# Fill products, tile forms, transfer order and norm-product places at the start and the block boundaries of a two-layer hybrid network

## The chip, the cores and the metric

The kernel runs on one core of one Trainium2 chip. The core has five engines that this text names by the profile's short names: PE (TensorE, matrix products), DVE (VectorE), ACT (ScalarE), POOL (GpSimd, idle here) and SP (SyncE, which issues every transfer here). Each works through its own queue in order, and they wait for each other by semaphores. The metric is device time in microseconds (us), the median of the timed runs; lower is better.

## The reference, cut to what matters

Two layers of a network with a latent sequence `x` and a context sequence `ctx`, 256 tokens of 1024 channels each. Each layer runs a feed-forward block, a mixer (a gated linear recurrence in layer 0, retention in layer 1) and a second feed-forward block. Ahead of each of them a norm is taken, scaled and shifted by vectors that come from a small product with the condition `c`:

```python
def modulate(h, shift, scale):
    return h * (1 + scale) + shift

def ada_mod(cond, w, b):
    m = jax.nn.silu(cond) @ w + b
    return jnp.split(m[..., None, :], N_MOD, axis=-1)
...
    for i in range(DEPTH):
        mx = ada_mod(c, mod_w[i], mod_b[i])
        mc = ada_mod(c_ctx, mod_w[i], mod_b[i])
        x = x + MACARON_W * mx[2] * swiglu(modulate(rms_norm(x, norm_g[i, 0]), mx[0], mx[1]),
                                           ffn_w_in[i, 0], ffn_w_out[i, 0])
        ...
        hx = modulate(rms_norm(x, norm_g[i, 1]), mx[3], mx[4])
        ...
        x = x + mx[5] * yx
        x = x + MACARON_W * mx[8] * swiglu(modulate(rms_norm(x, norm_g[i, 2]), mx[6], mx[7]),
                                           ffn_w_in[i, 1], ffn_w_out[i, 1])
    return rms_norm(x, final_g)
```

In the last layer only `x` is carried on after the mixer.

## The kernel before, in words

**Layout.** Channels lie on the 128 partitions, so `x` is 8 tiles (chunks) of 128x512: 256 context columns and 256 latent columns. All 371 weight tiles of 128x1024 (eight 128x128 blocks each) come in through SP in the order of use. A weight tile is split into a high part `whi` (ACT, L112) and a low part `wlo` (DVE, L138; some tiles are named `hhi`, `hlo`, since they are kept longer), and so is the input (`h`: ACT L348 writes the high half, DVE L354 the low half). A block of the product is three PE products: high by high (L142), high by low input (L143), low by high (L144).

**Modulation vectors.** `mod_order` lists 144 tiles of 128x1024, each worth 128 entries of one of nine vectors of a layer. A tile in form "V" is taken by DVE: two multiply-and-sum passes over 1024 columns (L242), one for each condition, and a small finishing operation (L265). A tile in form "P" is taken by PE: eight products of two columns each (L237, 16 entries in the trace), finished by two small operations on DVE (L262, L263). Vector 0 is the shift and vector 1 the scale of the first norm.

**The start** (`run`). SP issues the condition, the identity, `x` (8 transfers), then modulation and weight tiles. PE spreads the condition (L195), DVE sums the squares of `x` (`sq_acc`), PE sums them over the partitions (L296, in `stat`), DVE makes the inverse root in ten small operations (ends at L316), PE spreads it over the partitions (L329, `bcast`; "the broadcast" below). Then each chunk k of the normed input `h` is made by `h_chunk`: DVE (L346, scale), ACT (L348, shift and high half), DVE (L354, low half). A chunk needs its tile of vector 0 and of vector 1.

**The first product group** (`ffn` through `first_group`). Six accumulators stay open while PE goes through the eight chunks: 6 blocks of 3 products of 512 columns for a chunk, 18 in all (a "chunk's block" below). After chunk k's block a hook takes the two modulation tiles of chunk k+2 and makes `h` of chunk k+2.

**The block boundaries** (`boundary`, `out_proj`). After a block's output product the next norm is made while PE goes on. The context half's norm is made beside the latent half's output product; the latent half's `stat` and `bcast` lie in hooks of the next block's first group, which goes through the chunks twice with four accumulators: first the context columns (range 0), then the latent columns (range 1), 12 products of 256 columns for a chunk and range. A hook (r, k) runs after chunk k of range r. Four boundaries in the program have this form. Two, in the last layer after the mixer and at the program's end, carry only the latent half ("latent boundaries" below): there PE has nothing else to do, and `warm` fills it with products of a zero tile (L323), ten ahead of the broadcast, and six behind it at the first of the two.

**Order of the queues.** The order on each engine is that of the code. `w(key)` splits new weight tiles: the high part is issued at a tile's first block, the low part (`w_low`) when the blocks of the tile's second half begin. A small operation that is "pending" (`flush`) is issued by the next `h_chunk`.

Of the kernel before, what the change touches and what calls it, by code (L numbers as in the profile page):

```python
# [9 lines left out]
F32 = mybir.dt.float32  # L10
# [6 lines left out]
P = 128  # L17
# [26 lines left out]
def mod_order():  # L44

    out = []
    for k in range(KD):
        out.append((0, 0, k, "V", True))
        out.append((0, 1, k, "P", True))
# [25 lines left out]
class Kernel:  # L75
# [41 lines left out]
    def w(self, key, n=1):  # L117
# [9 lines left out]
        if o >= 4 or t == 0:  # L127
            self.w_low()
# [98 lines left out]
    def _tick(self):  # L227
# [6 lines left out]
        if form == "P":  # L234
# [4 lines left out]
            self.mod_finish(layer, idx, k, k + 1, 0, ps[:, 0:2])  # L239
        else:  # L240
# [5 lines left out]
            if (layer, idx) == (0, 0):  # L246
# [5 lines left out]
    def mod_finish(self, layer, idx, k0, k1, c0, src=None):  # L252
# [3 lines left out]
        ng = self.vec("ng").rearrange("p (l i k c) -> p l i k c", l=2, i=3, k=KD)  # L256
        if src is None:
            src = m
        else:
            src = src.rearrange("p (k c) -> p k c", k=k1 - k0)[:, :, c0:2]  # L260
# [15 lines left out]
    def sq_acc(self, st, d, c0, c1):  # L276

        nc = self.nc
# [4 lines left out]
        else:  # L283
            s = self.tmp("sq")
            nc.scalar.activation(s[:, :w], self.x[d][:, c0:c1], AF.Square)
            self.pend.append(lambda: nc.vector.tensor_tensor(st["acc"][:, :w], st["acc"][:, :w], s[:, :w],  # L286
                                                             ALU.add))

    def stat(self, s, ng, scale, between=None):
# [4 lines left out]
        ps = self.psum()  # L294
        for j in range(ng):
            nc.tensor.matmul(ps[:, j:j + 1], s[:, j * P:(j + 1) * P], self.ones, start=True, stop=True,  # L296
                             skip_group_check=True)
        if between:
            between()
# [59 lines left out]
    def out_proj(self, acts, key, layer, gidx, halves, st=None, hooks=None, tick=0, hold=False):  # L359
# [6 lines left out]
        for hi_, (c0, c1) in enumerate(halves):  # L366
# [14 lines left out]
            for d in range(KD):  # L381
# [6 lines left out]
                if st is not None and d:  # L388
                    self.sq_acc(st[hi_], d - 1, c0, c1)
                for c in range(2):  # L390
# [13 lines left out]
    def boundary(self, acts, key, layer, gidx, nl, nn, x_only=False, hold=False):  # L404
# [3 lines left out]
        if x_only:  # L408
            st = [{}]
            self.out_proj(acts, key, layer, gidx, [(T, 2 * T)], st=st)  # L410
            y = self.stat(st[0]["acc"], 2, 1.0 / D)
            self.warm(10)
# [19 lines left out]
        def hc(c, *ks):  # L432
            for k in ks:
# [4 lines left out]
        return {(0, 0): lambda: hc(0, 5, 6), (0, 1): lambda: (hc(0, 7), stat(1)), (0, 5): lambda: (bc(1), hc(1, 0)),  # L438
                (0, 6): lambda: hc(1, 1, 2), (0, 7): lambda: hc(1, 3, 4), (1, 0): lambda: hc(1, 5),
                (1, 1): lambda: hc(1, 6), (1, 2): lambda: hc(1, 7)}  # L440
# [528 lines left out]
    def run(self):  # L969
        nc, tc = self.nc, self.tc  # L970
        with ExitStack() as ctx:
# [27 lines left out]
            for k in range(1, 4):  # L999
                self.mod_prefetch(2 * k + 2, True)  # L1000
                self.w_fetch(k + 1)
# [5 lines left out]
            todo = self.spread_c()  # L1007
            st = {}
            for k in range(KD):
                self.sq_acc(st, k, 0, 2 * T)  # L1010
            self.flush()
            for o, ps in todo:
                nc.scalar.activation(o, ps, AF.Copy)
            y = self.stat(st["acc"], 4, 1.0 / D, self._tick)
            self._tick()
# [161 lines left out]
```

## Time and profile before

| what | before |
|---|---|
| median of 3 runs | 1885.56 us (1885.52 to 1885.7) |
| profiled execution, its own time | 1887.7 us |
| its span | 1885.9 us |
| mean granted PE clock | 0.991 |
| PE busy | 1857.2 us (98%), 10278 products |
| DVE busy | 1283.8 us (68%) |
| ACT busy | 718.2 us (38%) |
| HBM read | 274.80 MB, 146 GB/s over the span |

The profiled execution is 2.1 us longer than the median of the runs, and 1.8 us of its time lie outside its span. PE counts as busy while it works on anything, the fill included. The granted clock is 1 at 2.4 GHz and 0.5 at 1.2 GHz.

### The profile page before, as it was taken

How to read it: one execution, taken by the hardware profiler on the slowest of the kernel's cores; microseconds unless marked ns; L12 is line 12 of the kernel's file. 1: busy time of each engine (PE TensorE's matmuls, PEld its weight loads, DVE VectorE, ACT ScalarE, POOL GpSimd, SP SyncE). 2: the span in 40 equal slices, each digit the busy share in tenths (PEclk: the TensorE clock that was granted, in tenths of full speed). 3: DMA queues.
4: the chain of work that ended last, by engine and by line, in shares of the span. 5: the costliest groups of instructions: out<-in, count | busy, mean ns of one | idle time of the engine just before them, and what ended most of it. 6: DMA issues, size and time to landing. Idle time of an engine off the chain costs nothing.

```text
span 1885.9 us, 25731 instructions
## 1 busy us (share of the span) xinstructions
PE 1857.2 (98%) x10278; PEld 1621.5 (86%) x10278; DVE 1283.8 (68%) x2110; ACT 718.2 (38%) x984; POOL 0.2 (0%) x4
## 2 busy tenths in 40 slices
PE   8999999999999899999999999999999999999998
PEld 7888888897888888888889888888898899989997
DVE  7877697676899975767577655455576465675555
ACT  3322222248989342222224322222244243344442
POOL 0000000000000000000000000000000000000000
PEclk8999999999999999999999999999999999999999
DMA  8355454422322244454452445444324333355552
GB/s 319 127 211 187 167 189 181 145 90 79 100 90 90 79 157 168 158 185 172 143 172 94 154 150 187 145 171 178 102 80 150 124 123 118 97 160 182 176 186 101
DMA packets 77736, 277.52 MB, mean 147 GB/s; under 512 B 8752, under 2 KB 10032, under 8 KB 77616
## 3 DMA queue, kind: packets, MB, share of 16 engines
q1 hardware_dynamic: 77616, 275.88, 42.5%
q8 instruction: 80, 1.31, 0.3%
q14 instruction: 40, 0.33, 0.1%
HBM read 274.80 MB, written 1.05 MB: 146 GB/s over the span
## 4 chain that ended last, share of the span: by engine, by line
PE 92%; DVE 5%; ACT 1%; issue 1%; DMA 0%; SPq 0%; ACTq 0%; DVEq 0%
PE ps L142 30%; PE ps L144 30%; PE ps L143 30%; PE ps L237 1%; DVE x L393 1%; DVE wlo L138 1%; DVE hlo L138 1%; DVE h L354 0%; ACT h L348 0%; DVE acc L286 0%; PE ps L323 0%; PE ps L329 0%; PE ps L296 0%; DVE ht L346 0%; DMA x<-xt 0%
## 5 line engine op out<-in xcount | busy, mean ns | idle before, releaser
L142 PE MATMUL ps<-h,whi 128*128 128x512 f32 (+1 forms) x1824 | 641.1, 352 | 0.0
L144 PE MATMUL ps<-h,wlo 128*128 128x512 f32 (+1 forms) x1824 | 639.7, 351 | 1.2 <-DVE wlo L138 1.2
L143 PE MATMUL ps<-h,whi 128*128 128x512 f32 (+1 forms) x1824 | 640.3, 351 | 0.5 <-DVE h L354 0.5
L138 DVE TENSOR_TENSOR wlo<-wraw,whi 128x1024 fp32r<-128x1024 f32 x349 | 417.7, 1220 | 78.3 <-ACT whi L112 78.2
L112 ACT ACTIVATE whi<-wraw 128x1024 fp32r<-128x1024 f32 x349 | 357.3, 1050 | 275.8 <-PE ps L143 225.6
L144 PEld LDWEIGHTS ps<-h,wlo 128*128 128x128 f32 x1824 | 345.8, 190 | 47.7 <-DVE wlo L138 1.9
L143 PEld LDWEIGHTS ps<-h,whi 128*128 128x128 f32 x1824 | 345.9, 190 | 46.5 <-DVE h L354 1.6
L142 PEld LDWEIGHTS ps<-h,whi 128*128 128x128 f32 x1824 | 345.9, 190 | 44.9 <-ACT whi L112 0.3
L242 DVE SCALAR_TENSOR_TENSOR junk<-modraw,cB 128x1024 bf16<-128x1024 f32 x240 | 293.1, 1221 | 4.6
L393 DVE SCALAR_TENSOR_TENSOR x<-ps,M,x 128x256 f32<-128x256 f32 x296 | 132.5, 479 | 160.7 <-PE ps L144 160.3
L157 ACT ACTIVATE A<-sil 128x512 fp32r<-128x512 f32 (+1 forms) x88 | 50.9, 579 | 474.0 <-DVE sil L486 474.0
L142 PE MATMUL ps<-A,whi 128*128 128x512 f32 (+1 forms) x608 | 217.9, 358 | 0.0
L143 PE MATMUL ps<-A,whi 128*128 128x512 f32 (+1 forms) x608 | 217.9, 358 | 0.0
L144 PE MATMUL ps<-A,wlo 128*128 128x512 f32 (+1 forms) x608 | 217.9, 358 | 0.0
L486 DVE TENSOR_TENSOR sil<-ps,sil 128x512 f32<-128x512 f32 (+1 forms) x88 | 54.8, 623 | 159.8 <-PE ps L144 151.9
L144 PEld LDWEIGHTS ps<-A,wlo 128*128 128x128 f32 x608 | 114.9, 189 | 16.9
L143 PEld LDWEIGHTS ps<-A,whi 128*128 128x128 f32 x608 | 114.9, 189 | 16.9
L142 PEld LDWEIGHTS ps<-A,whi 128*128 128x128 f32 x608 | 114.9, 189 | 16.7
L158 DVE TENSOR_TENSOR A<-sil,A 128x512 fp32r<-128x512 f32 (+1 forms) x88 | 55.1, 626 | 56.7 <-ACT A L157 56.7
L485 ACT ACTIVATE sil<-ps 128x512 f32<-128x512 f32 (+1 forms) x88 | 47.3, 538 | 80.4 <-PE ps L144 79.9
L348 ACT ACTIVATE h<-ht,M 128x256 fp32r<-128x256 f32 x88 | 42.4, 504 | 91.5 <-DVE ht L346 91.5
L142 PE MATMUL ps<-A,hhi 128*128 128x256 f32 x192 | 54.8, 285 | 0.0
(171 smaller groups left out, 2065.3 us busy)
## 6 DMA issues: line engine op xcount, KB each, us to landing
wraw<-w SPq DMA_DIRECT2D x371, 512.0 KB, 4.3
modraw<-modw SPq DMA_DIRECT2D x144, 512.0 KB, 4.3
x<-xt SPq DMA_DIRECT2D x8, 256.0 KB, 4.9
mask<-mask SPq DMA_DIRECT2D x4, 512.0 KB, 6.0
out<-fin SPq DMA_DIRECT2D x8, 128.0 KB, 1.8
cs<-rope SPq DMA_DIRECT2D x1, 256.0 KB, 2.6
vecs<-vecs SPq DMA_DIRECT2D x1, 251.0 KB, 7.4
ident<-ident SPq DMA_DIRECT2D x1, 64.0 KB, 2.0
```

The source lines that it names most:

```text
L112: nc.scalar.activation(hi, raw, AF.Copy)
L138: self.nc.vector.tensor_tensor(lo, raw, hi.bitcast(F32), ALU.subtract)
L142: mm(ps, whi, xhi, start=first, stop=False, skip_group_check=True)
L143: mm(ps, whi, xlo, start=False, stop=False, skip_group_check=True)
L144: mm(ps, wlo, xhi, start=False, stop=last, skip_group_check=True)
L157: self.nc.scalar.activation(hi, src, AF.Copy)
L158: self.nc.vector.tensor_tensor(lo, src, hi.bitcast(F32), ALU.subtract)
L242: nc.vector.scalar_tensor_tensor(self.junk, raw, 1.0, self.cB[:, c, :], op0=ALU.mult, op1=ALU.mult, accum_out=M[:, idx, k, c:c + 1])
L348: nc.scalar.activation(h[:, 0, a:b], tt, AF.Identity, bias=M[:, 3 * n, k, c:c + 1])
L393: nc.vector.scalar_tensor_tensor(self.x[d][:, a0:a1], ps[:, a0 - c0:a1 - c0], M[:, gidx, d, c:c + 1], self.x[d][:, a0:a1], op0=ALU.mult, o ...
L485: nc.scalar.activation(s[:, :w], pa[:, c0:c1], AF.Silu)
L486: nc.vector.tensor_tensor(s[:, :w], pg[:, c0:c1], s[:, :w], ALU.mult)
```

## The change

**Forms.** Of the first 16 modulation tiles, vectors 0 and 1 of chunks 0 to 7 in turn, vector 0 was all "V" and vector 1 all "P". Now both tiles of chunks 0 and 1 are "P", chunks 2 to 5 are as before, and both tiles of chunks 6 and 7 are "V": eight of each form, as before. Finishing a tile of vector 1 takes one DVE operation (L260) in place of two, with `mb1` made ahead.

**The start.** On PE, 10, 3, 1 and 4 fill products stand between the spreading, the tile products, the norm products and the broadcast; the four tile products of chunks 0 and 1 all stand ahead of the first weight product, and the first of them ahead of the norm products. Of the transfers, modulation tiles 0 to 4 come ahead of weight tile 1 and 5 to 7 ahead of tile 2; in the hooks, tiles are fetched further ahead.

**The boundaries.** At the four two-half boundaries the latent `stat` moves from hook (0, 1) to (0, 2), the broadcast and the first chunk from (0, 5) to (0, 6), and the later chunks each by one hook. At the last chunk of an output product the pending sum of squares is issued ahead of the update of `x`. At the two latent boundaries the last chunk's squares are no longer added by DVE but summed by PE beside the others (two products accumulate), and the fill ahead of the broadcast is six instead of ten.

```diff
 def mod_order():
-        out.append((0, 0, k, "V", True))
-        out.append((0, 1, k, "P", True))
+        out.append((0, 0, k, "V" if k > 1 else "P", True))
+        out.append((0, 1, k, "P" if k < 6 else "V", True))
...
 def w(self, key, n=1):
-        if o >= 4 or t == 0:
+        if o >= 4:
             self.w_low()
...
 def _tick(self, late=None):
-            self.mod_finish(layer, idx, k, k + 1, 0, ps[:, 0:2])
+            f = lambda: self.mod_finish(layer, idx, k, k + 1, 0, ps[:, 0:2])
+            f() if late is None else late.append(f)
...
-            if (layer, idx) == (0, 0):
+            if layer == 0 and idx < 2:
                 self.mod_finish(layer, idx, k, k + 1, 0)
...
 def mod_finish(self, layer, idx, k0, k1, c0, src=None):
+        if layer == 0 and idx == 1:
+            nc.vector.tensor_scalar(m[:, 0], m[:, 0] if src is None else src, self.mb1[:, k0:k0 + 1],
+                                    ng[:, layer, 0, k0, 0:1], op0=ALU.add, op1=ALU.mult)
+            return
...
 def sq_acc(self, st, d, c0, c1):
+            if d == KD - 1 and st.get("two"):
+                st["last"] = s
+                return
...
 def stat(self, s, ng, scale):
+        parts = s if isinstance(s, list) else [s]
         for j in range(ng):
-            nc.tensor.matmul(ps[:, j:j + 1], s[:, j * P:(j + 1) * P], self.ones, start=True, stop=True,
-                             skip_group_check=True)
+            for i, s in enumerate(parts):
+                nc.tensor.matmul(ps[:, j:j + 1], s[:, j * P:(j + 1) * P], self.ones, start=i == 0,
+                                 stop=i == len(parts) - 1, skip_group_check=True)
...
 def out_proj(...):
                     self.sq_acc(st[hi_], d - 1, c0, c1)
+                    if d == KD - 1:
+                        self.flush()
...
 def boundary(...):
-            st = [{}]
+            st = [{"two": True}]
...
-            y = self.stat(st[0]["acc"], 2, 1.0 / D)
-            self.warm(10)
+            y = self.stat([st[0]["acc"], st[0]["last"]], 2, 1.0 / D)
+            self.warm(6)
...
-        return {(0, 0): lambda: hc(0, 5, 6), (0, 1): lambda: (hc(0, 7), stat(1)), (0, 5): lambda: (bc(1), hc(1, 0)),
-                (0, 6): lambda: hc(1, 1, 2), (0, 7): lambda: hc(1, 3, 4), (1, 0): lambda: hc(1, 5),
-                (1, 1): lambda: hc(1, 6), (1, 2): lambda: hc(1, 7)}
+        return {(0, 0): lambda: hc(0, 5, 6), (0, 1): lambda: hc(0, 7), (0, 2): lambda: stat(1), (0, 6): lambda: (bc(1), hc(1, 0)),
+                (0, 7): lambda: hc(1, 1, 2), (1, 0): lambda: hc(1, 3, 4), (1, 1): lambda: hc(1, 5),
+                (1, 2): lambda: hc(1, 6), (1, 3): lambda: hc(1, 7)}
...
 def run(self):
-            for k in range(1, 4):
-                self.mod_prefetch(2 * k + 2, True)
-                self.w_fetch(k + 1)
+            self.mod_prefetch(5, True)
+            self.w_fetch(2)
+            self.mod_prefetch(8, True)
...
             todo = self.spread_c()
+            self.warm(10)
...
-            y = self.stat(st["acc"], 4, 1.0 / D, self._tick)
-            self._tick()
+            late = []
+            self._tick(late)
+            y = self.stat(st["acc"], 4, 1.0 / D)
+            self.warm(3)
+            self._tick(late)
+            self.warm(1)
             rb = self.bcast(y, 4)
+            self.warm(4)
+            self.mb1 = self.const.tile([P, KD], F32, name="mb1")
...
+            for f in late:
+                f()
...
             h0(0)
             self.w_low()
+            self._tick()
+            self._tick()
+            h0(1)
...
                     if k + 2 < KD:
+                        self.mod_prefetch(min(2 * k + 10, 2 * KD), True)
                         self._tick()
                         self._tick()
                         h0(k + 2)
```

Three places show what moves. The lines of the changed kernel are 1 to 24 higher than those of before.

PE at the start, before, from the spreading (L195) to the first weight products (L142 to L144); L237 is the product of a modulation tile:

```order
L195 MATMUL ps<-ident,cT 128x128 x16
L296 MATMUL ps<-ones,acc 128x1 x4
L237 MATMUL ps<-cT,modraw 128x2 x8
L329 MATMUL ps<-ident,rs_y 128x128 x4
L237 MATMUL ps<-cT,modraw 128x2 x8
L142 MATMUL ps<-h_241,whi 128x512
```

The same with the change, from behind the ten fill products (L333; each is a pair of rows, and of three, one and four pairs one stands here); L238 is the tile product, L308 the norm product, L339 the broadcast:

```order
L238 MATMUL ps<-cT,modraw 128x2 x8
L308 MATMUL ps<-ones,acc 128x1 x4
...
L333 MATMUL ps<-warm_sb 128x512
L238 MATMUL ps<-cT,modraw 128x2 x8
L333 LDWEIGHTS warm_sb
L333 MATMUL ps<-warm_sb 128x512
L339 MATMUL ps<-ident,rs_y 128x128 x4
...
L238 MATMUL ps<-cT,modraw 128x2 x16
L142 MATMUL ps<-h_269,whi 128x512
```

Four tile products stand ahead of the first weight product where two stood, and the norm products stand behind the first of them.

DVE in the first group, before, for the two last chunks (`x_93`, `x_94`); L242 is one pass over a tile in form V:

```order
L242 SCALAR_TENSOR_TENSOR junk,M_85<-modraw,cB 128x1024 x2
L265 TENSOR_TENSOR M_85<-M_85,vecs 128x2
L262 SCALAR_TENSOR_TENSOR M_85<-ps,vecs 128x2
L263 TENSOR_TENSOR M_85<-M_85,vecs 128x2
L346 SCALAR_TENSOR_TENSOR ht<-x_93,M_85,ps 128x256 x2
L354 SCALAR_TENSOR_TENSOR h_514<-ht,M_85,h_514 128x256 x2
L242 SCALAR_TENSOR_TENSOR junk,M_85<-modraw,cB 128x1024 x2
L265 TENSOR_TENSOR M_85<-M_85,vecs 128x2
L262 SCALAR_TENSOR_TENSOR M_85<-ps,vecs 128x2
L263 TENSOR_TENSOR M_85<-M_85,vecs 128x2
L346 SCALAR_TENSOR_TENSOR ht<-x_94,M_85,ps 128x256 x2
L354 SCALAR_TENSOR_TENSOR h_563<-ht,M_85,h_563 128x256 x2
```

And with the change (L244 is the pass, L356 and L364 make `h`):

```order
L244 SCALAR_TENSOR_TENSOR junk,M_85<-modraw,cB 128x1024 x2
L271 TENSOR_TENSOR M_85<-M_85,vecs 128x2
L244 SCALAR_TENSOR_TENSOR junk,M_85<-modraw,cB 128x1024 x2
L260 TENSOR_SCALAR M_85<-M_85,mb_260,vecs 128x2
L356 SCALAR_TENSOR_TENSOR ht<-x_93,M_85,ps 128x256 x2
L364 SCALAR_TENSOR_TENSOR h_538<-ht,M_85,h_538 128x256 x2
L244 SCALAR_TENSOR_TENSOR junk,M_85<-modraw,cB 128x1024 x2
L271 TENSOR_TENSOR M_85<-M_85,vecs 128x2
L244 SCALAR_TENSOR_TENSOR junk,M_85<-modraw,cB 128x1024 x2
L260 TENSOR_SCALAR M_85<-M_85,mb_260,vecs 128x2
L356 SCALAR_TENSOR_TENSOR ht<-x_94,M_85,ps 128x256 x2
L364 SCALAR_TENSOR_TENSOR h_579<-ht,M_85,h_579 128x256 x2
```

Each of these two chunks has two tiles on DVE ahead of it where it had one.

DVE at a two-half boundary, before, from the end of the latent inverse root to the first latent chunks (`x0_87`, `x1_88`; the number behind a name is the buffer's):

```order
L316 SCALAR_TENSOR_TENSOR rs_y_3162<-rs_t_3161,rs_y_3162 128x2
L138 TENSOR_TENSOR hlo_3177<-wraw_2886,hhi_3176 128x1024
L138 TENSOR_TENSOR wlo_3207<-wraw_3111,whi_3206 128x1024
L346 SCALAR_TENSOR_TENSOR ht_3237<-x0_87,M0_85,ps_3234 128x256
L346 SCALAR_TENSOR_TENSOR ht_3257<-x1_88,M0_85,ps_3234 128x256
L354 SCALAR_TENSOR_TENSOR h0_3046<-ht_3237,M0_85,h0_3046 128x256
```

With the change:

```order
L326 SCALAR_TENSOR_TENSOR rs_y_3195<-rs_t_3194,rs_y_3195 128x2
L138 TENSOR_TENSOR hlo_3175<-wraw_2902,hhi_3174 128x1024
L138 TENSOR_TENSOR wlo_3223<-wraw_3127,whi_3222 128x1024
L356 SCALAR_TENSOR_TENSOR ht_3270<-x0_87,M0_85,ps_3267 128x256
L138 TENSOR_TENSOR wlo_3253<-wraw_3172,whi_3252 128x1024
L356 SCALAR_TENSOR_TENSOR ht_3286<-x1_88,M0_85,ps_3267 128x256
L364 SCALAR_TENSOR_TENSOR h0_3062<-ht_3270,M0_85,h0_3062 128x256
```

A weight tile's low part, which stood behind the second chunk, now stands between the first chunk's scaling and its low half (`h0`). On PE the broadcast stands one chunk later, with one chunk of range 0 (12 products) instead of two between it and the first product of range 1.

## Rows read from the trace of the kernel before

**Rows 1.** Stretches of the start: length, busy and count per engine, PEclk, DMA.

```profile
7.80:11.40 3.60, 0.00 (x1) 0.00 (x0) 2.55 (x4) 3.32 (x6) 0.00 (x0) 1.00 1.02 381
14.20:17.50 3.30, 3.30 (x17) 3.30 (x17) 2.40 (x13) 1.06 (x1) 0.00 (x0) 0.50 1.04 416
22.80:28.50 5.70, 5.70 (x15) 4.44 (x15) 4.92 (x12) 2.30 (x4) 0.00 (x0) 0.50 0.66 261
28.60:29.60 1.00, 1.00 (x6) 0.83 (x5) 1.00 (x2) 0.41 (x1) 0.00 (x0) 1.00 0.04 8
```

**Rows 2.** Timeline of PE, start to first group's end: start, us, what, [idle before].

```profile
12.47 1.86 PE L296 MATMUL ps<-ones,acc 128*128 128x1 f32 x8 [4.67 <-DVE acc L286]
14.20 3.55 PE L237 MATMUL ps<-cT,modraw 128*128 128x2 f32 x16
17.61 2.06 PE L329 MATMUL ps<-ident,rs_y 128*128 128x128 f32 x8
22.73 0.77 PE L142 MATMUL ps<-h,whi 128*128 128x512 f32 x1
...
59.27 1.84 PE L237 MATMUL ps<-cT,modraw 128*128 128x2 f32 x16
...
69.28 0.39 PE L142 MATMUL ps<-h,whi 128*128 128x512 f32 x1
```

**Rows 3.** Timeline of SP's queue around 11.8 us.

```profile
11.81 0.33 SPq L212 DMA_DIRECT2D modraw<-modw  x1
```

**Rows 4.** Timeline of DVE in the first group.

```profile
25.22 0.16 DVE L265 TENSOR_TENSOR M<-M,vecs 128x2 f32<-128x2 f32 x1
...
30.37 1.22 DVE L242 SCALAR_TENSOR_TENSOR junk<-modraw,cB 128x1024 bf16<-128x1024 f32 x1
...
58.59 1.22 DVE L242 SCALAR_TENSOR_TENSOR junk<-modraw,cB 128x1024 bf16<-128x1024 f32 x1
...
61.12 0.16 DVE L265 TENSOR_TENSOR M<-M,vecs 128x2 f32<-128x2 f32 x1
...
62.65 0.89 DVE L354 SCALAR_TENSOR_TENSOR h<-ht,M,h 128x256 fp32r<-128x256 f32 x2 [0.19 <-ACT h L348]
```

**Rows 5.** Timeline of PE at the first two-half boundary.

```profile
408.68 0.71 PE L329 MATMUL ps<-ident,rs_y 128*128 128x128 f32 x4 [0.41 <-DVE rs_y L316]
...
409.82 0.38 PE L144 MATMUL ps<-h,hlo 128*128 128x256 f32 x1 [0.20 <-DVE hlo L138]
...
412.55 0.28 PE L142 MATMUL ps<-h,whi 128*128 128x256 f32 x1
```

**Rows 6.** Timeline of DVE at the first two-half boundary.

```profile
408.54 1.23 DVE L138 TENSOR_TENSOR hlo<-wraw,hhi 128x1024 fp32r<-128x1024 f32 x1
409.69 1.22 DVE L138 TENSOR_TENSOR wlo<-wraw,whi 128x1024 fp32r<-128x1024 f32 x1
410.82 0.86 DVE L346 SCALAR_TENSOR_TENSOR ht<-x,M,ps 128x256 f32<-128x256 f32 x2
```

**Rows 7.** Timeline of PE at the two latent boundaries.

```profile
1675.56 0.61 PE L296 MATMUL ps<-ones,acc 128*128 128x1 f32 x4 [1.54 <-DVE acc L286]
1676.02 3.29 PE L323 MATMUL ps<-warm_sb 128*128 128x512 bf16 x10
1679.10 1.06 PE L329 MATMUL ps<-ident,rs_y 128*128 128x128 f32 x4
...
1878.53 0.65 PE L329 MATMUL ps<-ident,rs_y 128*128 128x128 f32 x4
```

**Rows 8.** Timeline of DVE at the two latent boundaries.

```profile
1677.98 0.16 DVE L316 SCALAR_TENSOR_TENSOR rs_y<-rs_t,rs_y 128x2 f32<-128x2 f32 x1
...
1876.68 0.16 DVE L316 SCALAR_TENSOR_TENSOR rs_y<-rs_t,rs_y 128x2 f32<-128x2 f32 x1
```

**Rows 9.** Stretches of the first latent boundary, columns as in rows 1.

```profile
1677.30:1680.60 3.30, 3.30 (x11) 1.85 (x10) 1.10 (x7) 0.00 (x0) 0.00 (x0) 0.50 0.00 0
1680.70:1684.00 3.30, 3.30 (x24) 2.69 (x22) 2.25 (x4) 1.86 (x3) 0.00 (x0) 1.00 0.00 0
```

More of the change, by code (lines that the diff above doesn't have):

```diff
@@ L225, in tick, with _tick @@
             self._tick()
-    def _tick(self):
+    def _tick(self, late=None):
         nc = self.nc
@@ L285, in sq_acc, with stat @@
             nc.scalar.activation(s[:, :w], self.x[d][:, c0:c1], AF.Square)
+            if d == KD - 1 and st.get("two"):
+                st["last"] = s
+                return
             self.pend.append(lambda: nc.vector.tensor_tensor(st["acc"][:, :w], st["acc"][:, :w], s[:, :w],
                                                              ALU.add))
-    def stat(self, s, ng, scale, between=None):
+    def stat(self, s, ng, scale):
         nc = self.nc
@@ L294, in stat @@
         ps = self.psum()
+        parts = s if isinstance(s, list) else [s]
         for j in range(ng):
-            nc.tensor.matmul(ps[:, j:j + 1], s[:, j * P:(j + 1) * P], self.ones, start=True, stop=True,
-                             skip_group_check=True)
-        if between:
-            between()
+            for i, s in enumerate(parts):
+                nc.tensor.matmul(ps[:, j:j + 1], s[:, j * P:(j + 1) * P], self.ones, start=i == 0,
+                                 stop=i == len(parts) - 1, skip_group_check=True)
         m = self.small.tile([P, 4], F32, tag="rs_m", name="rs_m")
@@ L1010, in run @@
                 self.sq_acc(st, k, 0, 2 * T)
-            self.flush()
+                self.flush()
             for o, ps in todo:
                 nc.scalar.activation(o, ps, AF.Copy)
-            y = self.stat(st["acc"], 4, 1.0 / D, self._tick)
-            self._tick()
-            rb = self.bcast(y, 4)
+            late = []
[4 more added lines that the diff above has]
+            self.warm(1)
+            rb = self.bcast(y, 4)
+            self.warm(4)
+            self.mb1 = self.const.tile([P, KD], F32, name="mb1")
+            mb = self.vec("mb").rearrange("p (l i k c) -> p l i k c", l=2, i=9, k=KD)
+            nc.vector.tensor_scalar(self.mb1, mb[:, 0, 1, :, 0], 1.0, None, op0=ALU.add)
+            for f in late:
+                f()
             self.h, self.hdone = [None] * KD, set()
@@ L1035, in mk @@
                 return f
-            self._tick()
-            self._tick()
-            h0(1)
             hooks = {(0, k): mk(k) for k in range(KD)}
```

## The prediction

> **What bounds the kernel now.** The table above has PE busy for 98% of the span, so a change counts only where it takes work or waiting out of PE's own queue, or where it puts some in. I read four places in this order: the granted clock and PE's queue up to the first weight product, DVE beside the first group, one two-half boundary, and the two latent boundaries.
>
> At the start PE stands idle from 7.8 us, since the sum of squares is not ready [rows 1, 2]: the norm products wait 4.67 us and begin at 12.47. The clock falls by 14.2 and stays at half until 28.5, through tile products that keep PE 100% busy (14.2 to 17.5), and through the first 5.7 us of real weight products (22.8 to 28.5) [rows 1]. The first group runs from 22.73 to 69.28 [rows 2]. Six of its steps hold a tile product; the last lasts from 59.27 to 60.97, 1.7 us. DVE is busy throughout: it starts on chunk 1's vectors at 25.22, on chunk 2's tile at 30.37, and ends the low half of the last chunk at 63.54 [rows 4]. PE takes up that chunk about 4.1 us (18 products of 0.23) ahead of 69.28, at 65.2. DVE is thus only 1.7 us early: it is nearly the second bound of this stretch, and that is what decides here.
>
> **The change part by part: the start.** The ten fill products run behind the spreading, from 7.8 to about 9.9 at full clock. Then PE waits for the first tile. Its transfer is done when the transfer eight places later, in the same slot, is issued: 11.81 [rows 3]. Its place in the queue is the same in the changed order. The tile product takes 1.7 at full clock, and then the norm products come, which so start at 13.5 instead of 12.47; at about 0.9 (half of the 1.86 of rows 2) they end at 14.4. The three fills end at 15.1.
>
> What the clock does is the main unknown. From 9.9 to 15 PE has a wait, two-column products and norm products, and 0.6 us of fill. In the trace of before, a pause of 3.6 us brought the clock down, and 3.3 us of PE at 100% on tile products did not bring it up [rows 1]; at the first latent boundary it fell too, after a pause of 1.54 us, norm products and some fill [rows 7, 9]. I take it that the clock falls by about 15. Then the second tile product takes 3.4 (14.20 to 17.61 [rows 2]) and ends at 18.5, one fill 0.43, the broadcast 2.0 [rows 2], four fills 1.7: 22.7. The inverse root is ready before (norm products' end 14.4 plus 2.0, which is 1677.98 + 0.16 less 1676.17 [rows 7, 8]). By then PE has had 4.1 us of fill and broadcast in a row. At the first latent boundary fill and broadcast from 1676.02 had the clock back after 1680.6, 4.6 us on [rows 7, 9]; behind 22.73 it came back 5.8 us on [rows 1, 2]. I take it that the clock is back about here, so that tiles 2 and 3 take 1.7 each and the weight products begin at **T = 26.1**. The bounds: T = 22.2 if the clock never falls (15.1 + 1.7 + 0.2 + 0.9 + 0.9 + 3.4, all of it at full), and T = 29.5 if it does not come back (22.7 + 6.8). The transfers do not decide: tile 3 comes two places behind tile 1, some 1.3 us for each of 512 KB at 416 GB/s [rows 1], well before 20.
>
> From T on DVE decides. It cannot begin chunk 1's vectors before the fourth tile product ends, at T. From there to chunk 2's tile it needs 5.1 (25.22 to 30.37 [rows 4]), and from there to the last low half 33.2 (30.37 to 63.54). The change adds a tile in form V for chunk 6 and one for chunk 7, 2.53 each (58.59 to 61.12), and saves a small operation in six steps, 0.2 each: 33.2 + 5.1 - 1.2 = 37.1. Then PE's last block takes 4.1. The first group ends at T + 0.1 + 5.1 + 37.1 + 4.1 = T + 46.4, which is 72.5 against 69.28: **+3.2** (bounds -0.7 and +6.6). So the two tile products taken out of PE's steps (3.4) gain nothing: PE then waits for DVE ahead of chunks 6 and 7, about 2.7 each time. A clock that falls in these waits would cost at most 1.7 behind the last one, which I leave in the range. What comes behind in DVE's queue is late too, but in before it frees accumulators that PE wants only after two more columns of 5.5 us.
>
> **The two-half boundaries.** PE waits there for DVE at the broadcast (0.41) and then for a low part (0.20) [rows 5]. That low part `hlo` is done at 408.54 + 1.23 = 409.77, and PE goes on at 409.82 [rows 5, 6]. In DVE's queue it stands behind the inverse root in either order, and the rows ahead of it do not move, so PE still passes this point at 409.82, whether the norm products come a chunk earlier or later. The earlier waits only run into this one. What moves is the broadcast: before, it lay in that shadow; now it comes behind the chunk, at about 411.1, and adds 0.46 to PE's queue. Its result is there some 0.75 later (0.71 [rows 5] and the signal), at 411.86. Then DVE does the first scaling (0.43, half of the 0.86), the low part that now stands between (1.13, from 409.69 to 410.82), the second scaling (0.39) and the first low half (0.45, half of 0.89 [rows 4]): 414.3. PE reaches the product that reads it at 413.2 (12 products of 0.12 behind the broadcast) and waits 1.1. Broadcast and wait make 1.6 for each of four such boundaries, as the row at the first stands for the others: **+6.4** (bounds 0, if DVE gets there earlier by something that I overlook, and +7.6 with 0.3 more each, for the square that DVE now adds only after its update of `x`). What is behind it, the weight products of the next block, moves by the same time.
>
> **The latent boundaries.** The inverse root is ready at 1678.14 and the broadcast starts at 1679.10; at the end, 1876.84 and 1878.53 [rows 7, 8]. The difference is the fill, which ran past the root at half clock. With six instead of ten the fill ends before. That gives back up to 1.0 and 1.7, plus some 0.2 each for the sum that DVE no longer makes; at the first, the six fills behind the broadcast can eat the gain. I take **-2.4** (bounds -0.5 and -3.2).
>
> **Sum.** 3.2 + 6.4 - 2.4 = +7.2 us. On the profiled execution's 1887.7 (1885.9 of span and 1.8 around it) that is 1894.9; the runs' median lies 2.1 lower, so 1885.56 + 7.2 = **1892.8 us**.
>
> **A rule weighed.** PE at 100% on tile products left the clock at half [rows 1]. The Trainium skill (TensorE: Matmul & The Clock Gate, Part 1: The HAM clock gate) says that a monitor sets the clock "based on how busy the PE has been recently". By that, a PE that never rests from 7.8 on but for 1.9 us would stay at full clock, and the first rival below would come true. The row is against it as far as it goes: it shows that tile products do not raise the clock, not that they cannot hold it.
>
> **The rivals.**
> - *The clock holds* (T = 22.2): -0.7 + 6.4 - 2.4 = +3.3, 1888.9, no difference that can be told. For it: the fill was absent in every pause in which the clock fell but the latent ones. Against: 0.6 us of fill in the five us from 9.9. It decides at T = 22.9, below which the start no longer loses. Chance 0.17.
> - *The clock does not come back* before the weight products (T = 29.5): +6.6 + 6.4 - 2.4 = +10.6, 1896.2. For it: behind 22.73 it came back only after 5.8 us of weight products. Chance 0.25.
> - *The boundaries cost nothing*: the first latent chunk's low half is ready when PE comes (by 413.2). Then +0.8, 1886.4. Against: the order of DVE's queue. Chance 0.12.
> - *The boundaries gain*: the waits of 0.41 and 0.20 vanish, and nothing follows: 4 x -0.6 = -2.4. With the start at T = 22.2 this is -5.5, 1880.1; at 26.1 it is -1.6. Against: they end in one wait on `hlo`, which does not move. Chance 0.10, most of it with the fast start.
>
> **How the numbers follow.** The forecast has 0.36. A measurement can tell about 0.2% (3.8 us). Slower by more: forecast and second rival, 0.61. Same: first and third, with the smaller part of the fourth, 0.31. Faster: 0.08. The range of 8 in 10 reaches from 1884.0, below the third rival, to 1897.5, the second with part of a clock that falls in DVE's waits. Below it lies most of the fourth (0.10), above it what several high bounds together would give (0.1).
>
> **What would show it.** The granted clock falls between 11 and 15 us and is up around 23; the first weight product is at 26; PE waits for `h` ahead of chunks 6 and 7; the first group ends near 72.5. At each two-half boundary PE waits about 1.1 for L364 at L143 ahead of range 1, and no longer at L339. At the end the broadcast starts within 0.2 of the root. I am wrong if the clock never falls, or if the wait ahead of range 1 is missing.

## The result and the profile after

The changed kernel takes 1898.7 us (median of 4 runs, 1896.69 to 1902.5) against 1885.63 in runs beside it: ratio 1.0071, 95% interval 1.0054 to 1.0089, 13 us slower. The forecast was 1892.8 with a range up to 1897.5: right in direction, too small. The profiled execution is the slowest of the four, 1902.5 (span 1900.7, 14.8 more than before's).

Each weight product is in both traces, so its shift tells where the time went in: at the first product behind the first group +10.8 (69.28 before, 80.05 after), +7.2 more over the four two-half boundaries and what lies between, -3.2 at the two latent boundaries. Forecast: +3.2, +6.4 and -2.4. The start is what failed.

Stretches of the start after, columns as in [rows 1]:

```profile
7.80:11.40 3.60, 2.68 (x15) 1.23 (x13) 3.19 (x5) 3.33 (x6) 0.00 (x0) 1.00 1.03 405
11.50:17.40 5.90, 5.50 (x28) 5.08 (x29) 1.79 (x9) 2.59 (x5) 0.00 (x0) 0.59 1.03 410
...
14.40:17.20 2.80, 2.58 (x11) 2.21 (x12) 0.84 (x6) 1.06 (x1) 0.00 (x0) 0.50 1.03 410
...
24.40:30.90 6.50, 6.50 (x33) 6.50 (x31) 1.69 (x3) 0.00 (x0) 0.00 (x0) 0.50 0.75 276
31.00:36.40 5.40, 5.40 (x14) 4.24 (x15) 4.54 (x8) 2.80 (x4) 0.00 (x0) 0.50 0.11 44
36.60:37.70 1.10, 1.10 (x6) 0.91 (x5) 1.06 (x3) 0.00 (x0) 0.00 (x0) 1.00 0.94 283
```

PE works nearly without a break from 11.7 us, but the clock falls inside the first tile product, at 12.6 (the second row's mean of 0.59 is 1.1 us at full clock and the rest at half), and is at half up to 36.4, 8 us longer than before [rows 1]. The timeline of PE after, against [rows 2]:

```profile
8.16 2.32 PE L333 MATMUL ps<-warm_sb 128*128 128x512 bf16 x10
11.69 2.76 PE L238 MATMUL ps<-cT,modraw 128*128 128x2 f32 x16 [1.21 <-DMA modraw<-modw]
14.31 1.84 PE L308 MATMUL ps<-ones,acc 128*128 128x1 f32 x8
...
17.25 3.41 PE L238 MATMUL ps<-cT,modraw 128*128 128x2 f32 x16
...
20.90 1.91 PE L339 MATMUL ps<-ident,rs_y 128*128 128x128 f32 x8
22.61 1.91 PE L333 MATMUL ps<-warm_sb 128*128 128x512 bf16 x4
24.31 6.83 PE L238 MATMUL ps<-cT,modraw 128*128 128x2 f32 x32
31.00 0.77 PE L142 MATMUL ps<-h,whi 128*128 128x512 f32 x1
...
68.22 0.50 PE L142 MATMUL ps<-h,whi 128*128 128x512 f32 x1 [2.51 <-ACT h L358]
...
75.54 0.50 PE L142 MATMUL ps<-h,whi 128*128 128x512 f32 x1 [2.65 <-ACT h L358]
...
80.05 0.39 PE L142 MATMUL ps<-h,whi 128*128 128x512 f32 x1
```

The last two early tiles take 6.83, not 3.4, and the weight products begin at 31.0, not 26.1. The two forecast waits ahead of chunks 6 and 7 are there. DVE in the same stretch, against [rows 4]:

```profile
31.18 0.28 DVE L260 TENSOR_SCALAR M<-ps,mb,vecs 128x2 f32<-128x2 f32 x1 [3.25 <-PE ps L238]
...
36.17 1.22 DVE L244 SCALAR_TENSOR_TENSOR junk<-modraw,cB 128x1024 bf16<-128x1024 f32 x1
...
39.65 0.28 DVE L260 TENSOR_SCALAR M<-ps,mb,vecs 128x2 f32<-128x2 f32 x1 [0.79 <-PE ps L238]
...
45.57 0.28 DVE L260 TENSOR_SCALAR M<-ps,mb,vecs 128x2 f32<-128x2 f32 x1 [1.06 <-PE ps L238]
...
75.12 0.89 DVE L364 SCALAR_TENSOR_TENSOR h<-ht,M,h 128x256 fp32r<-128x256 f32 x2 [0.19 <-ACT h L358]
```

DVE starts when the fourth tile product ends (31.18), as forecast, but then waits twice more for PE (0.79 and 1.06), since the first block ran at half clock and the tile product behind it came late.

The first two-half boundary, PE against [rows 5] and DVE against [rows 6]:

```profile
420.85 0.39 PE L144 MATMUL ps<-h,hlo 128*128 128x256 f32 x1 [1.32 <-DVE hlo L138]
...
422.14 0.60 PE L339 MATMUL ps<-ident,rs_y 128*128 128x128 f32 x4
...
425.25 0.39 PE L143 MATMUL ps<-h,whi 128*128 128x256 f32 x1 [0.95 <-DVE h L364]
```

```profile
419.57 1.23 DVE L138 TENSOR_TENSOR hlo<-wraw,hhi 128x1024 fp32r<-128x1024 f32 x1
420.71 1.22 DVE L138 TENSOR_TENSOR wlo<-wraw,whi 128x1024 fp32r<-128x1024 f32 x1
422.79 0.48 DVE L356 SCALAR_TENSOR_TENSOR ht<-x,M,ps 128x256 f32<-128x256 f32 x1 [0.86 <-PE ps L339]
423.19 1.22 DVE L138 TENSOR_TENSOR wlo<-wraw,whi 128x1024 fp32r<-128x1024 f32 x1
...
424.71 0.48 DVE L364 SCALAR_TENSOR_TENSOR h<-ht,M,h 128x256 fp32r<-128x256 f32 x1
```

The waits for L316's root and for `hlo` have run into one of 1.32; the broadcast waits for nothing and stands behind it; a new wait of 0.95 (1.23 from start to start, 424.02 to 425.25) is ahead of range 1. DVE now idles 0.86 for the broadcast.

The first latent boundary, PE and the end of the root on DVE, against [rows 7, 8]:

```profile
1694.09 1.24 PE L333 MATMUL ps<-warm_sb 128*128 128x512 bf16 x5
1696.04 0.71 PE L339 MATMUL ps<-ident,rs_y 128*128 128x128 f32 x4 [0.71 <-DVE rs_y L326]
```

```profile
1695.82 0.16 DVE L326 SCALAR_TENSOR_TENSOR rs_y<-rs_t,rs_y 128x2 f32<-128x2 f32 x1
```

The fill ends before the root, and the broadcast starts 0.06 behind it, where it stood 0.96 behind it before. In this run the clock stays full at both latent boundaries.

### The profile page after: what moved, and what is told of

It is laid out like the page before. It is cut to its first block, busy times and chain, and to the rows that moved or that the text cites. A ratio compares the mean times of both kernels' runs of the same rounds, so it can differ in the third digit from the quotient of the medians.

```text
span 1900.7 us, 25747 instructions
## 1 busy us (share of the span) xinstructions
PE 1861.0 (98%) x10293; PEld 1624.8 (85%) x10296; DVE 1283.6 (68%) x2101; ACT 718.5 (38%) x984; POOL 0.2 (0%) x4
## 4 chain that ended last, share of the span: by engine, by line
PE 90%; DVE 7%; ACT 2%; issue 1%; DMA 0%; SPq 0%; ACTq 0%; DVEq 0%
PE ps L144 29%; PE ps L143 29%; PE ps L142 29%; DVE wlo L138 1%; PE ps L238 1%; DVE junk L244 1%; DVE h L364 1%; DVE x L405 1%; ACT h L358 1%; DVE hlo L138 1%; DVE ht L356 1%; PE ps L339 0%; DVE acc L296 0%; PE ps L308 0%; DMA modraw<-modw 0%
## 5 line engine op out<-in xcount | busy, mean ns | idle before, releaser
L142 PE MATMUL ps<-h,whi 128*128 128x512 f32 (+1 forms) x1824 | 641.0, 351 | 5.2 <-ACT h L358 5.2
L144 PE MATMUL ps<-h,wlo 128*128 128x512 f32 (+1 forms) x1824 | 639.7, 351 | 1.2 <-DVE wlo L138 1.2
L142 PEld LDWEIGHTS ps<-h,whi 128*128 128x128 f32 x1824 | 345.9, 190 | 51.1 <-ACT h L358 6.3
L144 PEld LDWEIGHTS ps<-h,wlo 128*128 128x128 f32 x1824 | 345.7, 190 | 47.6 <-DVE wlo L138 1.9
L244 DVE SCALAR_TENSOR_TENSOR junk<-modraw,cB 128x1024 bf16<-128x1024 f32 x240 | 293.1, 1221 | 4.5
L142 PE MATMUL ps<-A,whi 128*128 128x512 f32 (+1 forms) x608 | 217.9, 358 | 0.0
L144 PE MATMUL ps<-A,wlo 128*128 128x512 f32 (+1 forms) x608 | 217.9, 358 | 0.0
L144 PEld LDWEIGHTS ps<-A,wlo 128*128 128x128 f32 x608 | 114.9, 189 | 16.9
L142 PEld LDWEIGHTS ps<-A,whi 128*128 128x128 f32 x608 | 114.9, 189 | 16.7
L292 ACT ACTIVATE sq<-x 128x256 f32<-128x256 f32 (+1 forms) x77 | 33.0, 433 | 57.9 <-DVE x L405 53.1
```

What stands on the lines that cost most here:

```text
L142: mm(ps, whi, xhi, start=first, stop=False, skip_group_check=True)
L144: mm(ps, wlo, xhi, start=False, stop=last, skip_group_check=True)
L244: nc.vector.scalar_tensor_tensor(self.junk, raw, 1.0, self.cB[:, c, :], op0=ALU.mult, op1=ALU.mult, accum_out=M[:, idx, k, c:c + 1])
```

## The experiments

**The four parts alone.** Each is the kernel before with one part of the change's diff. The start, all of it (e1_start: the diff without its pieces in `out_proj` and `boundary`, and without `two`):

> The kernel before with the whole change of the start alone. By the prediction's own term it is 3.2 us slower than before (1888.8). By the reading of the trace after, where the end of the first group lies 10.64 us later (65.42 + 10.64), it is about 10.6 us slower in a run like the profiled one and some us less in others, since the times after scatter over 5.8 us: 1891 to 1897, and it scatters over several us itself while the kernel before stays within 0.4. The rival, that the loss of the whole change comes mostly from the boundaries: under 4 us slower and no scatter.

1892.91 (1890.91 to 1896.68, 5 runs) against 1885.36: 1.0041 [1.0029, 1.0054]. The start is the larger loss and it scatters. In its profile the clock did come back about where the prediction had it:

```profile
19.84 1.92 PE L336 MATMUL ps<-ident,rs_y 128*128 128x128 f32 x8
21.54 1.91 PE L330 MATMUL ps<-warm_sb 128*128 128x512 bf16 x4
23.25 3.90 PE L238 MATMUL ps<-cT,modraw 128*128 128x2 f32 x32
27.01 0.60 PE L142 MATMUL ps<-h,whi 128*128 128x512 f32 x1
```

```profile
23.90:27.00 3.10, 3.10 (x29) 3.10 (x30) 1.12 (x2) 0.00 (x0) 0.00 (x0) 1.00 0.74 226
27.20:30.50 3.30, 3.30 (x9) 2.52 (x9) 2.62 (x6) 2.48 (x4) 0.00 (x0) 0.50 0.99 403
```

It came up behind broadcast and fill, at 23.8, so that the last two tiles took 3.90, and behind those tile products it fell again, under the first weight products. The trace after has the same broadcast and fill and no such return, so they alone don't bring it. PE was 100% busy in both rows. The first group still ended 5.8 us later than before (75.12), where the prediction's own formula for a beginning at 27.0 gives 4.1.

The two-half boundaries, whole and with the norm products alone moved:

```diff
 e2_bound
-        ... (0, 1): lambda: (hc(0, 7), stat(1)), (0, 5): lambda: (bc(1), hc(1, 0)), ...
+        ... (0, 1): lambda: hc(0, 7), (0, 2): lambda: stat(1), (0, 6): lambda: (bc(1), hc(1, 0)), ...
+                    if d == KD - 1:
+                        self.flush()
 e3_stat
+        ... (0, 1): lambda: hc(0, 7), (0, 2): lambda: stat(1), (0, 5): lambda: (bc(1), hc(1, 0)), ...
```

> The kernel before with the change of the four two-half boundaries alone (hooks moved, square issued earlier). Prediction: 4 x 1.6 = 6.4 us slower (1892.0), since the broadcast leaves the shadow of the wait on hlo and a new wait of 1.1 us stands ahead of range 1; the trace after has 7.3 us in the four places, 1.8 each. The rival (boundaries cost nothing of their own, and what the trace after shows there follows from the later start): within 1 us of before.

> The kernel before with only the norm products moved from hook (0, 1) to (0, 2) at the four two-half boundaries; the broadcast and the chunks stay where they were. If the waits end on hlo in either order and it is the broadcast's move that costs, this is within 1 us of before. If the later norm products make the inverse root late and this is the cost, it is 3 to 7 us slower. If the waits of 0.41 and 0.20 us go away with it, it is 1.6 to 2.4 us faster.

1892.24 (1891.85 to 1892.63; 1.0035 [1.0021, 1.0049]) and 1885.66 (1.0000 [0.9991, 1.0009]), both against 1885.36. The norm products' place costs nothing; the broadcast's and the chunks' place does. In the trace of the first the four boundaries shift the products by 1.67, 1.90, 1.66 and 1.64, 6.9 in all.

The latent boundaries alone:

```diff
 e4_latent
-            st = [{}]
+            st = [{"two": True}]
...
-            y = self.stat(st[0]["acc"], 2, 1.0 / D)
-            self.warm(10)
+            y = self.stat([st[0]["acc"], st[0]["last"]], 2, 1.0 / D)
+            self.warm(6)
```

> The kernel before with the change of the two latent boundaries alone (two products in place of the last addition, six fills in place of ten). Prediction: 2.4 us faster (1883.2), bounds 0.5 and 3.2; the trace after has 1.6 us at the first and 1.8 us at the end, 3.4 in all. The rival, that the gain in that trace came from a clock that happened not to fall there (the clock fell at both places before): under 1 us faster, or a time that scatters over 2 us between runs.

1883.88 (1882.11 to 1886.39) against 1885.36: 0.9990 [0.9982, 0.9999]. The profiles differ by 1.6 and 1.7 at the two places, but in that of before the clock fell at both and here at neither; the medians differ by half. What the change gives without a fall is seen in the profile of `f1_dense` (a run of the next part), which has ten fills here as before (L333 in its kernel) and whose clock stayed full at both places. PE, then DVE, at its first:

```profile
1677.81 2.10 PE L333 MATMUL ps<-warm_sb 128*128 128x512 bf16 x9
1679.76 0.71 PE L340 MATMUL ps<-ident,rs_y 128*128 128x128 f32 x4
```

```profile
1679.55 0.16 DVE L326 SCALAR_TENSOR_TENSOR rs_y<-rs_t,rs_y 128x2 f32<-128x2 f32 x1
```

There the ten fills hold nothing up: the root is ready at 1679.71 and the broadcast starts 0.05 behind it. From the last product ahead of this place to the first behind it PE takes 6.29, against 6.09 with the change (e4) and 7.67 in before. So without a fall the change gives 0.2 at each place, for the sum that DVE no longer makes; the rest is ten fills that run past the root because the clock fell. They did so at 11 of the 26 such places in the thirteen profiles with this part as before, by 0.95 to 1.73, and at none of the six with the change. Over thirteen profiles that is some 1.2 for each, and with twice 0.2 an estimate of 1.6, near the medians' 1.5. Whether the shorter fill also keeps the clock from falling is not shown.

The medians of the three parts add to 7.5 + 6.9 - 1.5 = 12.9, the whole loss. The start's other pieces (the order of the transfers, the place of the low parts in `w`) were not run alone.

**What in the start costs.** Four kernels, the first three from the start alone, the last from the kernel before:

```diff
 f1_dense (fill between the products of an early tile; without the fills behind the broadcast)
             for kc in range(KD):
                 nc.tensor.matmul(ps[:, 0:2], raw[:, kc * P:(kc + 1) * P], self.cT[:, kc, :], ...)
+                if kc % 2 == 0 and self.wps is not None:
+                    self.warm(1)
 f2_forms
-        out.append((0, 1, k, "P" if k < 6 else "V", True))
+        out.append((0, 1, k, "P", True))
 f3_nofill
-            self.warm(10)
-            self.warm(3)
-            self.warm(1)
-            self.warm(4)
 f4_fill (before, with f1's fill between the products)
+            self.warm(18)
...
             self._tick()
+            self.warm(2)
             rb = self.bcast(y, 4)
+            self.warm(2)
```

> The start of the change alone, with a fill product of 0.21 us (at full clock) behind every fourth of the sixteen two-column products of the four early tiles, and without the four fills behind the broadcast. Theory: two-column products do not hold the clock, fill between them does. Then PE goes at full clock from 11.6 on: 2.55 for each tile with its fill, 0.9 for the norm products, 1.0 for the broadcast, the weight products begin at about 24.6 (27.0 in the profile of the start alone) and at full clock, and the first group ends about 47.2 later: 2.5 us behind before, 1888. Rival (fill between them does not help, the clock comes and goes by other things): each tile takes 4.3 at half clock, the weight products begin at 31 or later, 1896 or more.

> The start of the change alone, but vector 1 of chunks 6 and 7 by PE again (ten tile products, six tiles on DVE). Theory (the late beginning of the weight products is the main loss, and PE's waits ahead of chunks 6 and 7 are only a little longer than the tile products that they replace): 1.5 to 2.5 us faster than the start alone, about 1891. Rival (the two more tiles on DVE are the main loss, 5.2 us of waiting in the trace after): 4 to 5 us faster, 1888.5. Rival 2 (the two tile products cost as much as the waits): within 0.7 us of the start alone.

> The start of the change alone, without its 18 fill products. Theory (the fill as placed does not keep the clock through the tile products, and itself takes 2 to 3 us of PE): the norm products' and tile products' 18 us at half clock begin at 11.6, the weight products begin at about 28.5, and the time is within 2 us of the start alone (1891 to 1895). Rival (the fill is what brings the clock back ahead of the last two tiles): 3 us or more slower, 1896.

> The kernel before with nothing but fill in its start: 18 fills behind the spreading (in the wait from 7.8 to 12.47), one behind every fourth of the two-column products of the two early tiles, two ahead of and two behind the broadcast. Theory: the clock is kept, the norm products end at 13.4, the broadcast follows the root (16.94 on DVE) and ends at 18.0, the first low half comes 1.6 us earlier, the weight products go at full clock, and DVE, 1.7 us early in before, ends the first group: 3.3 us faster than before, 1882. Rival (the clock falls all the same): 0 to 1 us slower.

| kernel | us (runs) | before | ratio |
|---|---|---|---|
| f1_dense | 1888.56 (1886.37 to 1900.29) | 1885.66 | 1.0027 [1.0011, 1.0043] |
| f2_forms | 1892.49 (1890.23 to 1894.93) | 1885.66 | 1.0034 [1.0021, 1.0046] |
| f3_nofill | 1892.83 (1892.74 to 1894.95) | 1885.66 | 1.0041 [1.0027, 1.0055] |
| f4_fill | 1884.68 (1883.13 to 1887.8) | 1885.66 | 0.9995 [0.9986, 1.0004] |

Without its 18 fills the start is as slow as with them: as placed, they bring nothing. With fill between the two-column products six of eleven runs took 1886.4 to 1888.6 and five 1893 to 1900. The profiled one kept the clock up to 58 us, past its first weight product at 23.40; then PE waited for chunk 6, and it fell up to 64.8:

```profile
58.59 0.80 PE L143 MATMUL ps<-h,whi 128*128 128x512 f32 x1 [3.03 <-ACT h L359]
```

In the kernel before the same fill kept the clock full up to 618.9 us in the profile, and the first group ended at 66.03, 3.25 us earlier than in the profile of before, as expected (3.3). But 1882 was expected, and the median is 1884.68, only 1.0 below that of before: the five other profiles with the start of before (e2, e3, e4, g3, g4) end the first group anywhere from 67.76 to 69.82, so 69.28 is one of the late ones. With the forms of before for chunks 6 and 7 (f2), 1.5 to 2.5 us were expected back and 0.4 came: the weight products of its profile began at 29.33 instead of 27.01. So this pair doesn't tell what the forms cost.

**Combined, and the boundary taken apart.**

```diff
 g1_best = f4_fill with e4_latent;  g2_dense_forms = f1_dense with f2_forms
 g3_noflush = e2_bound without
-                    if d == KD - 1:
-                        self.flush()
 g4_lowfirst = e2_bound with
-        ... (0, 6): lambda: (bc(1), hc(1, 0)), ...
+        ... (0, 6): lambda: (bc(1), hc(1, 0), self.flush()), ...
```

> The kernel before with the dense fill of its start and the change of the two latent boundaries, the only two edits that measured at or below before (1.0 and 1.5 us faster by their medians). If they add: about 1883, 2.5 us faster than before. If the first leaves the clock in another phase at the latent boundaries, so that the second gains nothing there: about 1884.5, as the fill alone.

> The start of the change with the dense fill, and with vector 1 of chunks 6 and 7 by PE again. Where the clock holds, PE waited 3.0 us ahead of chunk 6 with the dense fill and the clock then fell from 58.0 to 64.8. Theory (with the clock held, the two more tiles on DVE are what is left of the loss, and their wait brings the clock down again): no wait there, the first group ends about 2 us ahead of before, 1884, and the runs scatter less than the 14 us of the dense fill. Rival (the four tile products ahead of the first weight product are the loss): as the dense fill alone, 1888.

> The change of the two-half boundaries without the part that issues the pending work ahead of the last update of x. In the trace after, that update comes 0.87 us later against its neighbours and the low parts hlo 0.39 us later than in before. If that part is the cause: 4 x 0.38 = 1.5 us faster than the whole change of these boundaries, 1890.7. If the later hlo follows from the moved hooks: the same, 1892.2.

> The change of the two-half boundaries, but with the low half of the first latent chunk issued right behind its scaling, ahead of the weight tile's low part wlo. Theory (PE's wait of 1.23 us ahead of range 1 is that wlo's 1.13 us on DVE): the wait shrinks to 0.2 or so, 4 x 1.0 = 4 us faster than the whole change of these boundaries, 1888.2. Rival (the late broadcast alone makes the first latent chunk late): within 1 us of 1892.2.

| kernel | us (runs) | before | ratio |
|---|---|---|---|
| g1_best | 1882.53 (1882.33 to 1886.18) | 1885.96 | 0.9983 [0.9974, 0.9992] |
| g2_dense_forms | 1894.01 (1889.97 to 1896.1) | 1885.96 | 1.0041 [1.0028, 1.0053] |
| g3_noflush | 1890.55 (1889.08 to 1892.69) | 1885.96 | 1.0024 [1.0015, 1.0033] |
| g4_lowfirst | 1892.54 (1891.62 to 1894.72) | 1885.96 | 1.0037 [1.0024, 1.0049] |

The two edits add up, and a little more: 3.4 us faster than before, with a clock of 0.998 over the profile. The second expectation failed, but not by its rival: the clock fell at 14.5 and stayed at half to 34.9, though PE's queue up to the weight products is that of f1_dense. This stretch of the two profiles, f1_dense first:

```profile
17.30:20.60 3.30, 3.22 (x30) 3.16 (x30) 1.62 (x5) 0.91 (x2) 0.00 (x0) 1.00 1.02 406
```

```profile
17.30:20.60 3.30, 3.30 (x17) 3.03 (x18) 0.08 (x2) 0.00 (x0) 0.00 (x0) 0.50 1.03 408
```

The third came out as expected: without the pending work ahead of `x` the four boundaries shift the products by 5.7 instead of 6.9 in the traces, and the medians are 1.7 apart. The fourth refutes my reason for the wait ahead of range 1. DVE, then PE, at its first such boundary:

```profile
411.38 0.48 DVE L346 SCALAR_TENSOR_TENSOR ht<-x,M,ps 128x256 f32<-128x256 f32 x1 [0.86 <-PE ps L329]
412.44 0.48 DVE L354 SCALAR_TENSOR_TENSOR h<-ht,M,h 128x256 fp32r<-128x256 f32 x1 [0.58 <-ACT h L348]
412.84 1.22 DVE L138 TENSOR_TENSOR wlo<-wraw,whi 128x1024 fp32r<-128x1024 f32 x1
413.98 0.87 DVE L346 SCALAR_TENSOR_TENSOR ht<-x,M,ps 128x256 f32<-128x256 f32 x2
```

```profile
412.98 0.39 PE L143 MATMUL ps<-h,whi 128*128 128x256 f32 x1
...
415.05 0.38 PE L142 MATMUL ps<-h,whi 128*128 128x256 f32 x1 [0.49 <-ACT h L348]
```

The first low half comes ahead of `wlo` and PE's gap there shrinks to 0.37, but `wlo` now delays the second chunk, where gaps of 0.77 and 0.52 appear. In this trace the four boundaries shift the products by 8.1, against 6.9 in e2's. DVE has the same work to do from the late broadcast on, whatever stands first.

**Is the clock held by enough fill?** Eight fills for each early tile in place of four, with either set of forms:

```diff
 h1_denser_p = g2_dense_forms, h2_denser_v = f1_dense, both with
-                if kc % 2 == 0 and self.wps is not None:
+                if self.wps is not None:
```

> As the dense fill with ten tile products, but a fill behind every second of the two-column products, eight for each early tile instead of four. Theory A (the clock is held by fill if there is enough of it; four for a tile are on the edge): the clock stays full in all runs, each tile takes 3.4, the weight products begin at 27.9 and the first group ends 43.0 later (eight blocks of 4.1 and six tile products of 1.7), 1.6 us behind before: 1887, within 3 us of each other. Theory B (fill between two-column products does not hold the clock, it held by chance): the clock is at half in most profiles, each tile takes 6.8, the weight products begin at 40, 1900 or more.

> The same with the forms of the change (two tiles on DVE for chunks 6 and 7). With the clock held, the first group ends 47.0 behind the first weight product, as in the profile with the dense fill (23.40 to 70.4): 5.6 us behind before, 1891, and 4 us slower than with ten tile products. If the two more tiles on DVE cost nothing beyond the tile products that they replace: the same as with ten tile products. Theory B of the clock: 1900 or more.

1887.01 (1885.26 to 1894.87, 11 runs; 1.0008 [0.9999, 1.0017]) and 1889.84 (1888.28 to 1891.76, 10 runs; 1.0020 [1.0011, 1.0030]), against 1885.74. Nine of eleven runs of the first lie within 2.3 us at a mean clock of 0.996 to 0.998, as theory A has it; the other two, at 1894, are at 0.993. The profile of one of these shows a longer pause ahead of the first tile, and the clock at half from 15.0:

```profile
13.11 0.38 PE L239 MATMUL ps<-cT,modraw 128*128 128x2 f32 x2 [3.15 <-DMA modraw<-modw]
```

The second stayed within 3.5 us in all runs, its profile at full clock up to 69.3. So denser fill held the clock in most runs; that the long wait lost it in the one profiled is a guess from a single trace. The start then costs 1.3 us with ten tile products and 4.1 with the forms of the change, fill included. Against the 7.5 of the start alone, 3.4 or more went with the clock (an estimate from medians). And two more tiles on DVE cost about 3 us, in two waits of PE (5.5 us in all, the longer 2.9):

```profile
PE ps L143 <- ACT h L359: 5.5, 2, 2.9
```

## Why the prediction was off

**The start, +3.2 forecast, +10.8 in the profile (7.5 in medians): this step failed.** "I take it that the clock is back about here, so that tiles 2 and 3 take 1.7 each and the weight products begin at T = 26.1" did not hold: that the clock falls was right, though at 12.6 and not by 15; the return was not. T came out at 31.0, beyond the upper bound of 29.5, which still had the first tile at full clock: 1.6 us were lost up to the last two tiles (24.31 for 22.7) and 3.3 in them. In this profile the second rival, with 0.25, was the case. The prediction's own signs of being wrong (no fall of the clock, no wait ahead of range 1) did not cover it. The formula T + 46.4 was 2.65 short too (31.00 to 80.05 is 49.05): it has DVE busy throughout, and left out DVE's two waits for late tile products, 1.85 together, which follow from the half clock under the first block; and it counted too much for the small operations, with a saving of 0.06 for each small operation left out (57.34 to 57.74 for what took from 56.27 to 56.73), not 0.2. 3.2 + 4.9 + 2.65 = 10.75. In e1's profile T was nearly right (27.0) and the formula still 1.7 short, with one such wait of 0.95.

The runs bear the mechanism out: where the clock was held in the changed start (f1 in six runs, h1 in nine, by their mean clocks), the time fell to what was expected of a held clock, and the versions that lost it lie at 1890 to 1900. In the kernel before (f4) the trace shows that gain and the median a third of it. What was wrong was to treat one return of the clock, at a latent boundary, as a delay that could be carried over: e1's profile has it back at 23.8, after's at 36.4, with the same queue on PE up to there. That the two more tiles on DVE take back what PE saves was right, and h1 against h2 shows it: they take some 3 us more.

**The two-half boundaries, +6.4: right in size, half right in reason.** Measured 6.9 alone and 7.2 in the trace. The broadcast left the shadow of `hlo`, the wait ahead of range 1 is 1.23 (1.1 forecast), and e3 shows that the norm products' place is free. Two details were wrong. `hlo` "does not move" held with the hooks alone (0.01 us against the products around it in g3's trace), but with the pending work issued ahead of `x` at the first boundary it came 0.25 us later, and PE with it, near the 0.3 that I had put into the bound for that part. And putting the low half ahead of that `wlo` did not shorten the boundary (g4). What is left is the later place of the broadcast and of the chunks behind it, which e3 left where they were; no run moved one without the other.

**The latent boundaries, -2.4: between the measured values**, -3.2 in the trace and -1.5 alone. The fill past the root was the right reason, but the prediction took from its one trace that the clock falls there, and it does so in part of the profiles only; without a fall no more than the 0.2 each for the sum is left. So the size came out near by an average that was not forecast.

**The rule weighed.** In the rows of after from 14.40 to 36.40 PE is over 90% busy, at half clock. That stays against my reading of the Trainium skill (TensorE: Matmul & The Clock Gate, Part 1: The HAM clock gate) that a PE which hardly rests keeps its clock. From 17.30 to 20.60 it was as busy at full clock in f1_dense (3.22 of 3.30) as at half in g2_dense_forms and in after (3.30 of 3.30), so its busy share in these rows does not tell the two apart.

## What to carry to other kernels

A stretch of tiny products like this one should be priced at half clock, unless a trace shows the clock at full under just these products. Fill in blocks beside them brought nothing here (f3 against e1); fill between them held the clock in most runs, the denser the more often, and takes PE time of its own. When two engines are within 2 us of each other, work moved from one to the other must be priced on the receiver at its full length. A step moved later in a queue costs nothing while its readers wait for something else in any case (the norm products, e3); moved out of that shadow it delays everything that reads its result, and reordering what is behind it (g4) didn't give that back. And a gain that one trace shows where the clock fell should be looked for in a trace where it did not.

## What was unexpected of the hardware

Two profiles with the same queue on PE, and the same times to within 0.12 us from 11.6 to 14.0, had a clock of 1.00 and of 0.50 from 14.5 on (f1_dense and g2_dense_forms). Ahead of it they differ little: PE's spreading took 5.44 and 5.86 us, and its wait ahead of the first tile 0.76 and 0.23. Runs of one kernel differ too, so whether the clock falls in such a stretch isn't fixed by the program alone, and a kernel with such a stretch scatters (14 us in f1_dense, 3.5 in h2_denser_v, which held the clock). What else decides is open. And the clock fell under full-width weight products too (e1_start, 27.2), right behind tile products that ran at full clock.
